# Attention gate and output projection of a two-layer trunk: order of the last gate tiles, of the output-weight splits and of the contraction blocks

## The chip, the cores and the metric

The kernel runs on one core of a Trainium2 chip. The metric is the device time of one execution in microseconds (us). Three executions of the kernel before took 1691.3 to 1694.68 us, their median is 1691.89 us. The profile comes from another execution.

## The reference

The program is a decoder trunk of two layers over 1024 tokens of width 1024, in float32. What the change touches is the end of layer 0:

```python
# layer 0: dilated attention, three dilation groups, 16 heads of 64
outs, lses = [], []
for g, (window, dilation) in enumerate(((128, 1), (512, 4), (2048, 16))):
    o, l = dilated_group_attention(q[g], k[g], v[g], rel_bias, window, dilation)
    outs.append(o); lses.append(l)
wts = softmax(stack(lses), axis=0)            # merge of the three groups
o = sum(wts[..., None] * stack(outs), axis=0)
h = (o * silu(z)) @ w_out                     # gate, then output projection
x = x + rms_norm(h, post_norm)
# layer 1: gated state-space layer, the same frame
```

The gate input z is a projection of the normalised input, like q, k and v.

## The kernel before

Each float32 operand of a large product is split into a rounded high part and a low part (`split`, L79: a copy on ScalarE, L83, and a subtraction on VectorE, L84), and each product is three matmuls: high by high, high by low, low by high. The contraction over 1024 goes in eight blocks k of 128.

Heads go in eight pairs p of 128 channels. For each pair the three groups are projected, attended and merged; the merge weights come from the row maxima and sums (`merge_weights`, L604: a load of them as tile `cm` at L609, small VectorE operations and an exponential on ScalarE, L612 to L620, and a store to `wt_dr`), and are loaded again as `mw` by `weights_of`. For pairs 0 to 6 the merge runs on GpSimd (`merge`, L684 to L690) and leaves the result in `on_dr`. For the last pair `merge_last` (L694) does it on VectorE, on tiles that are in SBUF.

The gate is projected in channel tiles p of 128 and token halves th of 512. Tiles 4 to 7 are projected early, in the first phase, and stored; the merges of pairs 4 to 6, and the last merge by L703, multiply by them. Tiles 0 to 3 are projected in `attn_gate`, whose work stands among and behind that of the last pair: `in_order` runs (0,0), (0,1), (1,0), (1,1), (2,0), (2,1), (3,0), (3,1). Each step makes a SiLU (`silu2`: tanh on ScalarE at L803, a product on VectorE at L804, tile `tz`), loads the merged heads (`fz`, L833), multiplies the two on GpSimd (L834) and splits the product into `gh` and `gl`. A gate product for half th fills half the columns of every token tile, so a block k is complete when both halves are done. Beside the first three steps `early` loads and splits blocks 4, 5 and 6 (L824). The tiles `tz` and `fz` come from one ring of seven slots under two tags (3 and 4), taken in turn by `slot`.

The output projection (`attn_out`, `out_tiles`) computes eight token tiles i by two column halves n. Its weights are loaded as `wo` (L815) and split into `woh` and `wol`. These tiles take the space of the attention's activations: column half 0 that of token half 0 (high parts under tag a0, low parts under a2), column half 1 that of token half 1 (a1 and a3). So a split of the weights of half n can begin only when the last projection has read token half n. `out_tiles` begins with four groups, (0,0), (1,0), (0,1), (1,1), over blocks 0 to 6, then adds block 7 to each, then takes the other tiles one by one, with the post norm (`out_norm`) and the next layer's normalised transposes beside them.

All loads and stores are issued on SyncE's queue. Every engine runs its queue in order. The order on each queue is made before the launch by a planner, which simulates the program with its own durations and takes what is ready, program order and the priority of `high_priority` deciding; so an instruction may stand elsewhere than the source has it. `issue_after(x)` makes it place an instruction behind x.

Of the kernel before, what the change touches and what calls it, by code (L numbers as in the profile page):

```python
# [18 lines left out]
AF = mybir.ActivationFunctionType  # L19
ALU = mybir.AluOpType  # L20
# [6 lines left out]
KT = 8  # L27
# [4 lines left out]
AHEAD = 600  # L32

EARLY = 4


ORD = (1, 4, 8)
# [41 lines left out]
def split(c, hi, lo, src, scale=None, engine=None):  # L79

    nc = c.nc
    if scale is None:
        nc.scalar.copy(hi, src)  # L83
        return (engine or nc.vector).tensor_tensor(lo, src, f32(hi), op=ALU.subtract)  # L84
    else:
        nc.scalar.activation(hi, src, AF.Copy, scale=scale)
        nc.vector.scalar_tensor_tensor(lo, src, scale, f32(hi), op0=ALU.mult, op1=ALU.subtract)
# [513 lines left out]
        nc.sync.dma_start(bass.AP(dr.tensor, off + n * 1024, dims), md[8 * n:8 * n + 8])  # L601


def merge_weights(c, p):  # L604

    nc = c.nc
    cm, e, d = c.compact
    src = bass.AP(c.ms_dr.tensor, c.ms_dr.offset + p * 3 * 4096, [[32, 64], [2048, 6], [1, 32]])
    nc.sync.dma_start(cm.rearrange("p g m n -> p (g m) n"), src)  # L609
    m, s = cm[:, :, 0], cm[:, :, 1]  # L610
    mx, den = d[:, 0], d[:, 1]
    nc.vector.tensor_tensor(mx, m[:, 0], m[:, 1], op=ALU.max)  # L612
    nc.vector.tensor_tensor(mx, mx, m[:, 2], op=ALU.max)
    nc.vector.tensor_tensor(e, m, mx.unsqueeze(1).to_broadcast([64, 3, 32]), op=ALU.subtract)
    nc.scalar.activation(e, e, AF.Exp)
    nc.vector.tensor_tensor(s, s, e, op=ALU.mult)
    nc.vector.tensor_tensor(den, s[:, 0], s[:, 1], op=ALU.add)
    nc.vector.tensor_tensor(den, den, s[:, 2], op=ALU.add)
    nc.vector.reciprocal(den, den)
    nc.vector.scalar_tensor_tensor(e, e, 0.5, den.unsqueeze(1).to_broadcast([64, 3, 32]), op0=ALU.mult, op1=ALU.mult)  # L620
    off = c.wt_dr.offset + p * 3 * 2048
    nc.sync.dma_start(bass.AP(c.wt_dr.tensor, off, [[32, 64], [2048, 3], [1, 32]]), e)
# [16 lines left out]
def attn_pair(c, p, w_in, h):  # L639
    nc = c.nc  # L640
    c.pair = p
    O = []
    for g in range(3):
        qh = c.attn.tile([P, S], F32R, tag="qh", name="qh", bufs=2)
        ql = c.attn.tile([P, S], F32R, tag="ql", name="ql", bufs=2)
        w = load_w(c, w_in[g * 8 + p])
        for th in range(2):
            src = proj_half(c, w, h[th])
            with c.tc.high_priority(AHEAD):
                evac_q(c, src, g, th * H, (qh, ql))  # L650
# [12 lines left out]
        ms = c.small.tile([P, 32], F32, tag="ms", name="ms")  # L663
        for u in range(2):
            attn_unit(c, g, u, (qh, ql), (kh, kl), v, bt, ms, O)
            if p and g == u == 0:
                merge_weights(c, p - 1)
    if p == 7:
        merge_weights(c, p)
        c.last = O  # L670
    c.merge = lambda: merge(c, p, O)

# [21 lines left out]
def merge_last(c, O, w):  # L694

    nc = c.nc
    for g in range(3):
        nc.vector.tensor_tensor(O[g], O[g], w[g], op=ALU.mult)
        if g:
            nc.vector.tensor_tensor(O[g], O[g], O[g - 1], op=ALU.add)  # L700
    g7 = c.wraw.tile([P, S], F32, tag="wraw", name="mg")
    nc.sync.dma_start(g7, c.g_dr[7])
    nc.vector.tensor_tensor(O[2], O[2], g7, op=ALU.mult)  # L703
    return O[2]
# [94 lines left out]
def silu2(c, t, ps):  # L799

    nc = c.nc
    with c.tc.high_priority(AHEAD):
        nc.scalar.activation(t, ps, AF.Tanh, scale=0.5)  # L803
        nc.vector.scalar_tensor_tensor(t, t, 1.0, ps, op0=ALU.add, op1=ALU.mult)  # L804


def attn_gate(c, a, h):
# [9 lines left out]
    def early(p):  # L817
        load_out(p, 0)
        for i in range(2):
            if p == 7:  # L820
                f = merged[:, i * H:i * H + H]
            else:
                f = c.slot("fz")
                nc.sync.dma_start(f, c.on_dr[p, :, i * H:i * H + H])  # L824
            split(c, g[i][0][:, p, :], g[i][1][:, p, :], f)

    def use(p, th, ps):
        if th == 0:
            load_out(p, 0)
        t = c.slot("tz")  # L830
        silu2(c, t, ps)
# [9 lines left out]
    def step(t):  # L841
        if t < 7 - EARLY:
            early(EARLY + t)
        c.wide = int(t >= 3)
        if t == 2 * EARLY - 2:
            with c.tc.high_priority(AHEAD):
                weights.extend(weights_of(c, 7, g) for g in range(3))

    in_order(c, [a["w_in"][48 + p] for p in range(EARLY)], h, use, step)
    c.wide = c.banks = 0  # L850
    merged = merge_last(c, c.last, weights)
    early(7)
    for p in range(8):
        load_out(p, 1)
    return g, raw
# [2 lines left out]
def out_part(c, ps, g, w, i, n, ks):  # L858
# [2 lines left out]
    gh, gl = g[i // 4]  # L861
    wh, wl = w[n]
    ts = slice(i % 4 * P, i % 4 * P + P)
    for k in ks:
        nc.tensor.matmul(ps, gh[:, k, ts], wh[:, k, :], start=k == 0, stop=False)  # L865
        nc.tensor.matmul(ps, gh[:, k, ts], wl[:, k, :], start=False, stop=False)  # L866
        nc.tensor.matmul(ps, gl[:, k, ts], wh[:, k, :], start=False, stop=k == KT - 1)  # L867


def out_bank(c, i):  # L870
# [1 line left out]
    return pool.tile([P, H], F32, tag=tag, name="pso")  # L872


def out_half(c, g, w, i, n):

    ps = out_bank(c, i)
    out_part(c, ps, g, w, i, n, range(KT))
    return ps


# [28 lines left out]
        done(ns)  # L910


def out_tiles(c, g, w, post, res, done, late=0, last=None):


    pss = [[None] * 2 for _ in range(8)]
    split_k = KT - 1 if late else KT
    order = [(0, 0), (1, 0), (0, 1), (1, 1)] if late < 3 else [(i, n) for n in range(2) for i in range(late)]
    for i, n in order:
        pss[i][n] = out_bank(c, i)  # L920
        out_part(c, pss[i][n], g, w, i, n, range(split_k))
    ahead = max(2, late)
    for i in range(8):
        if late and i == 0:
            for j in range(ahead):
                for n in range(2):
                    out_part(c, pss[j][n], g, w, j, n, (KT - 1,))
        elif i + 1 >= ahead and i < 7:
            for n in range(2):
                pss[i + 1][n] = out_half(c, g, w, i + 1, n)  # L930
# [16 lines left out]
def attn_out(c, a, g, raw):  # L947
# [527 lines left out]
def trunk(tc, a):  # L1475
# [6 lines left out]
    with ExitStack() as es:  # L1482
# [61 lines left out]
        for n in range(2):  # L1544
            for k in range(KT):
# [5 lines left out]
        out_tiles(c, y2, w, post, lambda i: c.x1_dr[i], lambda i, x: nc.sync.dma_start(ov[i], x), 2,  # L1551
                  lambda x, ns: nc.sync.dma_start(ov[7][:, ns], x[:, ns]))


# [88 lines left out]
```

## Time and profile before

| What | Value |
|---|---|
| median of 3 runs | 1691.89 us |
| profiled execution | 1692.35 us |
| its span, first to last instruction | 1690.6 us |
| mean granted TensorE clock | 0.991 |
| TensorE matmul, busy | 1655.9 us (98%) |
| VectorE, busy | 1012.3 us (60%) |
| ScalarE, busy | 712.8 us (42%) |
| GpSimd, busy | 452.8 us (27%) |

Times in the trace are microseconds from the start of the span. PE is TensorE's matmul, PEld its weight load, DVE VectorE, ACT ScalarE, POOL GpSimd, SP SyncE, which issues the transfers. A granted clock of 1.00 is TensorE's full speed. In rows of instructions, "out<-in" are the kernel's tiles, and a bracket or a last column tells how long the engine stood idle before it and who ended that. Merged rows (x6) give the start of the first and the time to the end of the last.

### The profile page before, as it was taken

What the parts mean: (1) busy time and instruction counts of PE and PEld (TensorE: products, weight loads), DVE (VectorE), ACT (ScalarE), POOL (GpSimd) and SP (SyncE); (2) the same over time, 40 slices, a digit from 0 to 9 for tenths busy, and PEclk for the clock granted to TensorE, in tenths of its full rate; (3) what the DMA queues carried; (4) which work ended last, traced back from release to release, by engine and by line L of the source; (5) the groups of instructions that cost most, each with busy time, mean ns of one, the idle gap of its engine ahead of it and who ended that gap; (6) DMA issues with size and microseconds to landing.
All of it is one profiled execution on the core that took longest, in us unless ns stands there. A gap on an engine that the chain in (4) does not pass through costs nothing.

```text
span 1690.6 us, 26330 instructions
## 1 busy us (share of the span) xinstructions
PE 1655.9 (98%) x9714; PEld 1395.1 (83%) x9714; DVE 1012.3 (60%) x2511; ACT 712.8 (42%) x1730; POOL 452.8 (27%) x301
## 2 busy tenths in 40 slices
PE   8999999999999999999999999998999999999998
PEld 6889999978888888888888888886888887867886
DVE  8698898625454554545455454567462788845533
ACT  5232232226456464646556464654352222243411
POOL 2000000132241514324252523303220344513121
PEclk9999999999999999999999999998999999989999
DMA  6222455531232423233142323228146978365432
GB/s 238 83 55 101 148 176 163 166 105 54 89 104 65 118 69 98 83 93 92 58 136 71 110 83 101 87 69 225 63 155 195 262 223 250 112 206 164 147 119 87
DMA packets 176857, 212.19 MB, mean 126 GB/s; under 512 B 37443, under 2 KB 133462, under 8 KB 176728
## 3 DMA queue, kind: packets, MB, share of 16 engines
q1 hardware_dynamic: 176728, 210.52, 41.7%
q8 instruction: 76, 1.25, 0.3%
q14 instruction: 53, 0.43, 0.1%
HBM read 153.51 MB, written 56.96 MB: 124 GB/s over the span
## 4 chain that ended last, share of the span: by engine, by line
PE 85%; DVE 7%; DMA 4%; issue 1%; POOL 1%; ACT 1%; SPq 0%; DVEq 0%; POOLq 0%; ACTq 0%
PE psj L110 45%; PE psq L373 10%; PE psl L471 5%; PE pso L548 4%; PE pt L499 4%; PE pso L865 3%; PE pso L866 3%; PE pso L867 3%; PE psb L110 1%; PE pso L574 1%; DVE T L1366 1%; DMA fz<-on_dr 1%; PE psv L234 1%; PE psv L233 1%; PE psv L232 1%
## 5 line engine op out<-in xcount | busy, mean ns | idle before, releaser
L110 PE MATMUL psj<-hh,whi 128*128 128x512 f32 x896 | 358.1, 400 | 0.0
L110 PE MATMUL psj<-hh,wlo 128*128 128x512 f32 x896 | 358.1, 400 | 0.0
L110 PE MATMUL psj<-hl,whi 128*128 128x512 f32 x896 | 355.2, 396 | 0.0
L84 POOL TENSOR_TENSOR wlo<-wraw,whi 128x1024 fp32r<-128x1024 f32 x48 | 115.2, 2400 | 394.8 <-ACT whi L83 379.7
L110 PEld LDWEIGHTS psj<-hh,whi 128*128 128x128 f32 x896 | 168.8, 188 | 37.0
L110 PEld LDWEIGHTS psj<-hh,wlo 128*128 128x128 f32 x896 | 168.8, 188 | 36.4
L110 PEld LDWEIGHTS psj<-hl,whi 128*128 128x128 f32 x896 | 168.7, 188 | 36.3
L488 ACT ACTIVATE lg<-lg,nm 128x128 f32<-128x128 f32 (+1 forms) x384 | 168.2, 442 | 37.0 <-DVE nm L483 37.0
L477 DVE CUSTOM_DVE_ANT_0 lg<-psl,T 128x128 f32<-128x128 f32 (+1 forms) x384 | 110.6, 347 | 89.1 <-PE psl L471 89.1
L83 ACT CAST whi<-wraw 128x1024 fp32r<-128x1024 f32 x80 | 83.7, 1046 | 161.9 <-PE psj L110 108.0
L373 PE MATMUL psq<-whi,v 128*128 128x256 f32 x640 | 120.3, 284 | 0.0
L110 PE MATMUL psj<-h1h,whi 128*128 128x512 f32 (+1 forms) x272 | 104.9, 386 | 1.1 <-ACT h1h L83 1.1
L84 DVE TENSOR_TENSOR ph<-pt,ph 128x512 fp32r<-128x512 f32 (+2 forms) x160 | 96.7, 622 | 15.3 <-ACT ph L83 13.1
L84 DVE TENSOR_TENSOR kl<-psj,kh 128x512 fp32r<-128x512 f32 x48 | 33.2, 691 | 119.3 <-ACT kh L83 118.8
L110 PE MATMUL psj<-h1l,whi 128*128 128x512 f32 (+1 forms) x272 | 104.2, 383 | 0.2 <-DVE h1l L84 0.2
L110 PE MATMUL psj<-h1h,wlo 128*128 128x512 f32 (+1 forms) x272 | 104.0, 383 | 0.0
L83 ACT CAST ph<-pt 128x512 fp32r<-128x512 f32 (+2 forms) x160 | 81.5, 529 | 46.5 <-PE pt L499 45.5
L373 PEld LDWEIGHTS psq<-whi,v 128*128 128x128 f32 x640 | 100.0, 189 | 1.2 <-issue 1.2
L373 PE MATMUL psq<-wlo,v 128*128 128x256 f32 x320 | 91.2, 285 | 0.7 <-DVE wlo L84 0.7
L548 PE MATMUL pso<-ph,vs 128*128 128x256 f32 (+1 forms) x544 | 86.6, 284 | 0.0
L499 PE MATMUL pt<-identr,lg 128*128 128x128 f32 x560 | 82.2, 276 | 0.0
L1232 POOL TENSOR_TENSOR Ks<-Ks,O 128x16 f32<-128x16 f32 x8 | 4.3, 536 | 284.5 <-ACT Ks L1230 284.5
(284 smaller groups left out, 3691.0 us busy)
## 6 DMA issues: line engine op xcount, KB each, us to landing
wraw<-in_w_in_dram SPq DMA_DIRECT2D x56, 512.0 KB
mw<-wt_dr SPq DMA_DIRECT2D x48, 256.0 KB
v<-in_w_v_dram SPq DMA_DIRECT2D x20, 512.0 KB
vp<-v_dr SPq DMA_DIRECT2D x16, 512.0 KB
wraw<-in_ssm_w_in_dram SPq DMA_DIRECT2D x16, 512.0 KB
v_dr<-v SPq DMA_DIRECT2D x30, 256.0 KB
rot_dr<-rt SPq DMA_DIRECT2D x48, 128.0 KB
ca_dr<-ca SPq DMA_DIRECT2D x32, 144.0 KB
```

What stands on the lines that cost most here:

```text
L83: nc.scalar.copy(hi, src)
L84: return (engine or nc.vector).tensor_tensor(lo, src, f32(hi), op=ALU.subtract)
L110: nc.tensor.matmul(ps, a[:, s], b[:, k, :], start=first and k == 0 and n == 0, stop=k == KT - 1 and n == 2, skip_group_check=True)
L373: nc.tensor.matmul(o, r[x][:, k, ts], w[y][:, k, :], skip_group_check=True, start=i in (0, 4, 5) and t % 2 == k == n == 0, stop=k == 3 and ...
L471: nc.tensor.matmul(psl[:, h, o], x[HEADS[h], qs], y[HEADS[h], ks], start=j == js[0] and n == 0, stop=n == 2, skip_group_check=True)
L477: nc.vector.tensor_tensor_reduce(lg[:, h, j, 0:w], psl[:, h, o], bt[:, h, 256 - w:256], scale=1.0, scalar=-3.0e38, op0=ALU.add, op1=ALU.ma ...
L488: nc.scalar.activation(lg[:, h, j, 0:w], lg[:, h, j, 0:w], AF.Exp, bias=nm[:, h, b:b + 1], accum_out=ms[:, col:col + 1])
L499: c.nc.tensor.transpose(pt[:, n * P:(n + 1) * P], lg[:, h, j, part * P:part * P + P], c.ident)
L548: nc.tensor.matmul(o, l, r, start=n == 0, stop=n == len(jobs) - 1, skip_group_check=True)
L865: nc.tensor.matmul(ps, gh[:, k, ts], wh[:, k, :], start=k == 0, stop=False)
L866: nc.tensor.matmul(ps, gh[:, k, ts], wl[:, k, :], start=False, stop=False)
L867: nc.tensor.matmul(ps, gl[:, k, ts], wh[:, k, :], start=False, stop=k == KT - 1)
```

## The change

It has five parts. The merge weights of the last pair: their load stays, the arithmetic moves into the second gate step, behind the splits of block 5. The gate steps run in the order (0,0), (0,1), (1,0), (1,1), (2,0), (3,0), (2,1), (3,1). The splits of the output weights go through the blocks in the order 4, 5, 6, 0, 1, 2, 3, 7, and those of column half 1 are placed behind the last SiLU. The output projection contracts in the same order of blocks, and its first four groups run over six blocks, with blocks 3 and 7 added after. The two additions of the last merge go to GpSimd. The output projection of layer 1 is called with the plain order of blocks and a split of seven and one, as it was before.

```diff
+K_GATED = (4, 5, 6, 0, 1, 2, 3, 7)
+K_ORDER = tuple(range(8))
...
-        nc.scalar.copy(hi, src)
+        c.last_hi = nc.scalar.copy(hi, src).ins
...
+def merge_load(c, p):
     cm, e, d = c.compact
     src = bass.AP(c.ms_dr.tensor, c.ms_dr.offset + p * 3 * 4096, [[32, 64], [2048, 6], [1, 32]])
-    nc.sync.dma_start(cm.rearrange("p g m n -> p (g m) n"), src)
+    c.nc.sync.dma_start(cm.rearrange("p g m n -> p (g m) n"), src)
...
     if p == 7:
-        merge_weights(c, p)
+        merge_load(c, p)
         c.last = O
...
         if g:
-            nc.vector.tensor_tensor(O[g], O[g], O[g - 1], op=ALU.add)
+            nc.gpsimd.tensor_tensor(O[g], O[g], O[g - 1], op=ALU.add)
...
-            split(c, g[i][0][:, p, :], g[i][1][:, p, :], f)
+            c.early_lo = split(c, g[i][0][:, p, :], g[i][1][:, p, :], f).ins
...
+        if t == 1:
+
+            with c.tc.issue_after(c.last_hi), c.tc.issue_after(c.early_lo):
+                merge_weights(c, 7)
...
-    in_order(c, [a["w_in"][48 + p] for p in range(EARLY)], h, use, step)
+    ws = {}
+    for t, (p, th) in enumerate(((0, 0), (0, 1), (1, 0), (1, 1), (2, 0), (3, 0), (2, 1), (3, 1))):
+        if th == 0:
+            ws[p] = load_w(c, a["w_in"][48 + p])
+        use(p, th, proj_half(c, ws[p], h[th]))
+        step(t)
     c.wide = c.banks = 0
     merged = merge_last(c, c.last, weights)
     early(7)
+    c.gates_done = c.silu
...
-    for k in ks:
-        nc.tensor.matmul(ps, gh[:, k, ts], wh[:, k, :], start=k == 0, stop=False)
+    for n, k in ks:
+        nc.tensor.matmul(ps, gh[:, k, ts], wh[:, k, :], start=n == 0, stop=False)
...
     for n in range(2):
-        for k in range(KT):
-            split(c, w[n][0][:, k, :], w[n][1][:, k, :], raw[n][:, k, :])
+        with ExitStack() as es:
+            if n:
+                for i in c.gates_done:
+                    es.enter_context(c.tc.issue_after(i))
+            for k in K_GATED:
+                split(c, w[n][0][:, k, :], w[n][1][:, k, :], raw[n][:, k, :])
...
-    out_tiles(c, g, w, post, lambda i: xv[i], done, 2)
+    out_tiles(c, g, w, post, lambda i: xv[i], done, K_GATED, 2)
```

## Rows read from the trace of the kernel before

**Rows 1.** The page: busy time by engine (us, share of the span, instructions), and the chain of work that ended last, by engine.

```profile
PE 1655.9 (98%) x9714; PEld 1395.1 (83%) x9714; DVE 1012.3 (60%) x2511; ACT 712.8 (42%) x1730; POOL 452.8 (27%) x301
...
PE 85%; DVE 7%; DMA 4%; issue 1%; POOL 1%; ACT 1%; SPq 0%; DVEq 0%; POOLq 0%; ACTq 0%
```

**Rows 2.** TensorE's groups of instructions from 1154.3 to 1261.9: line, tiles, shapes, count, then busy us, mean ns of one, idle us just before them and who ended it. `pso` is the output projection, `pst` the transposes.

```profile
L866 PE MATMUL pso<-wol,gh 128*128 128x512 f32 x128 | 52.9, 414 | 3.0 <-DVE wol L84 3.0
L865 PE MATMUL pso<-woh,gh 128*128 128x512 f32 x128 | 52.6, 417 | 3.9 <-ACT gh L83 3.9
L867 PE MATMUL pso<-woh,gl 128*128 128x512 f32 x128 | 49.9, 401 | 0.7 <-DVE gl L84 0.7
L127 PE MATMUL pst<-identr,xn 128*128 128x128 f32 x48 | 6.2, 272 | 0.0
```

**Rows 3.** Stretches of the span: bounds, length, then busy us (instructions) of PE, PEld, DVE, ACT and POOL in this order, the granted TensorE clock, the share of the 16 DMA engines, and GB/s.

```profile
1154.03:1261.95 107.92, 100.21 (x435) 80.38 (x434) 62.76 (x203) 47.15 (x108) 28.34 (x20) 0.95 0.39 128
1143.05:1154.25 11.20, 11.20 (x49) 9.01 (x48) 7.77 (x9) 4.47 (x9) 3.45 (x3) 1.00 1.11 247
1110.00:1130.00 20.00, 20.00 (x127) 16.94 (x127) 9.96 (x29) 11.94 (x40) 3.30 (x2) 1.00 0.05 15
1139.00:1171.00 32.00, 28.24 (x114) 21.98 (x113) 28.12 (x40) 16.52 (x33) 8.62 (x5) 0.95 1.10 309
...
1158.90:1162.10 3.20, 3.20 (x9) 2.47 (x9) 3.20 (x5) 2.91 (x7) 0.64 (x1) 0.50 1.02 382
1176.80:1182.50 5.70, 5.69 (x13) 4.51 (x14) 0.81 (x3) 0.27 (x1) 0.00 (x0) 0.50 0.00 0
```

**Rows 4.** TensorE's instructions in order of time, at full clock: start us, us, line, tiles. Between these two starts stand two further matmuls.

```profile
1183.58 0.40 PE L866 MATMUL pso<-wol,gh 128*128 128x512 f32 x1
...
1184.28 0.40 PE L866 MATMUL pso<-wol,gh 128*128 128x512 f32 x1
```

**Rows 5.** The chain of waits in order of time, around the gate and the output projection: start us, us, what.

```profile
1131.62 2.57 DMA cm<-ms_dr
...
1145.52 7.56 DMA fz<-on_dr
...
1163.83 7.30 DMA fz<-on_dr
...
1176.36 0.41 ACT gh L83
...
1178.04 0.43 PE pso L865
...
1209.17 0.87 PE pst L127 x8
```

**Rows 6.** ScalarE's instructions in order of time: start us, us, line, tiles, shapes, count, idle time before and who ended it.

```profile
1134.93 0.28 ACT L615 ACTIVATE cm<-cm 64x96 f32<-64x96 f32 x1 [2.76 <-DVE cm L614]
...
1135.37 3.41 ACT L83 CAST gh<-fz 128x256 fp32r<-128x256 f32 x8
```

**Rows 7.** GpSimd's instructions in order of time, the same columns.

```profile
1110.15 1.69 POOL L834 TENSOR_TENSOR fz<-fz,tz 128x512 f32<-128x512 f32 x1 [38.24 <-DVE tz L804]
1120.36 1.61 POOL L834 TENSOR_TENSOR fz<-fz,tz 128x512 f32<-128x512 f32 x1 [8.53 <-DVE tz L804]
...
1171.29 5.03 POOL L834 TENSOR_TENSOR fz<-fz,tz 128x512 f32<-128x512 f32 x2 [11.75 <-DMA fz<-on_dr]
```

**Rows 8.** VectorE's instructions in order of time, the same columns.

```profile
1137.47 3.15 DVE L84 TENSOR_TENSOR gl<-fz,gh 128x512 fp32r<-128x512 f32 x6
...
1152.35 1.22 DVE L698 TENSOR_TENSOR O<-O,mw 128x1024 f32<-128x1024 f32 x1
...
1156.69 6.41 DVE L84 TENSOR_TENSOR wol<-wo,woh 128x512 fp32r<-128x512 f32 x7
...
1172.19 1.28 DVE L84 TENSOR_TENSOR gl<-O,gh 128x512 fp32r<-128x512 f32 x2
1175.32 2.29 DVE L84 TENSOR_TENSOR gl<-fz,gh 128x256 fp32r<-128x256 f32 x4 [1.85 <-ACT gh L83]
```

**Rows 9.** Transfers issued on SyncE's queue, in order of time: start us, us of the issue, line, tiles, count.

```profile
1122.00 0.34 SPq L824 DMA_DIRECT2D fz<-on_dr  x1
...
1137.40 0.33 SPq L824 DMA_DIRECT2D fz<-on_dr  x1
...
1146.87 4.86 SPq L833 DMA_DIRECT2D fz<-on_dr  x2
...
1163.83 1.82 SPq L833 DMA_DIRECT2D fz<-on_dr  x2
```

**Rows 10.** Durations of single operations, by line or tile: ns min/median/max, first and last start us, shapes.

```profile
L83 ACT CAST woh<-wo x16: 612/618/627, 1151.9 to 1163.9; 128x512 fp32r<-128x512 f32 x16
...
L84 DVE TENSOR_TENSOR wol<-wo,woh x16: 675/677/2067, 1156.7 to 1171.6; 128x512 fp32r<-128x512 f32 x16
...
L700 DVE TENSOR_TENSOR O<-O,O x2: 1226/1900/2574, 1151.2 to 1153.6; 128x1024 f32<-128x1024 f32 x2
...
L834 POOL TENSOR_TENSOR fz<-fz,tz x8: 1516/1738/3557, 1110.1 to 1174.8; 128x512 f32<-128x512 f32 x8
...
L824 SPq DMA_DIRECT2D fz<-on_dr x6: 319/380/600, 877.4 to 1139.8; - x6
...
L686 POOL TENSOR_TENSOR O<-O,O x14: 2387/2393/2404, 477.8 to 1063.2; 128x1024 f32<-128x1024 f32 x14
```

More of the change, by code (lines that the diff above doesn't have):

```diff
@@ L601, in put_ms @@
         nc.sync.dma_start(bass.AP(dr.tensor, off + n * 1024, dims), md[8 * n:8 * n + 8])
+def merge_load(c, p):
+    cm, e, d = c.compact
+    src = bass.AP(c.ms_dr.tensor, c.ms_dr.offset + p * 3 * 4096, [[32, 64], [2048, 6], [1, 32]])
+    c.nc.sync.dma_start(cm.rearrange("p g m n -> p (g m) n"), src)
 def merge_weights(c, p):
@@ L607, in merge_weights @@
     cm, e, d = c.compact
-    src = bass.AP(c.ms_dr.tensor, c.ms_dr.offset + p * 3 * 4096, [[32, 64], [2048, 6], [1, 32]])
-    nc.sync.dma_start(cm.rearrange("p g m n -> p (g m) n"), src)
     m, s = cm[:, :, 0], cm[:, :, 1]
@@ L666, in attn_pair @@
             if p and g == u == 0:
+                merge_load(c, p - 1)
                 merge_weights(c, p - 1)
     if p == 7:
-        merge_weights(c, p)
+        merge_load(c, p)
         c.last = O
@@ L802, in silu2 @@
     with c.tc.high_priority(AHEAD):
-        nc.scalar.activation(t, ps, AF.Tanh, scale=0.5)
-        nc.vector.scalar_tensor_tensor(t, t, 1.0, ps, op0=ALU.add, op1=ALU.mult)
+        return (nc.scalar.activation(t, ps, AF.Tanh, scale=0.5).ins,
+                nc.vector.scalar_tensor_tensor(t, t, 1.0, ps, op0=ALU.add, op1=ALU.mult).ins)
 def attn_gate(c, a, h):
@@ L830, in use @@
         t = c.slot("tz")
-        silu2(c, t, ps)
+        c.silu = silu2(c, t, ps)
         f = c.slot("fz").rearrange("p (i n) -> p i n", i=8)
@@ L863, in out_part @@
     ts = slice(i % 4 * P, i % 4 * P + P)
-    for k in ks:
-        nc.tensor.matmul(ps, gh[:, k, ts], wh[:, k, :], start=k == 0, stop=False)
+    for n, k in ks:
+        nc.tensor.matmul(ps, gh[:, k, ts], wh[:, k, :], start=n == 0, stop=False)
         nc.tensor.matmul(ps, gh[:, k, ts], wl[:, k, :], start=False, stop=False)
-        nc.tensor.matmul(ps, gl[:, k, ts], wh[:, k, :], start=False, stop=k == KT - 1)
+        nc.tensor.matmul(ps, gl[:, k, ts], wh[:, k, :], start=False, stop=n == KT - 1)
 def out_bank(c, i):
@@ L872, in out_bank, with out_half @@
     return pool.tile([P, H], F32, tag=tag, name="pso")
-def out_half(c, g, w, i, n):
+def out_half(c, g, w, i, n, ks):
     ps = out_bank(c, i)
-    out_part(c, ps, g, w, i, n, range(KT))
+    out_part(c, ps, g, w, i, n, ks)
     return ps
@@ L910, in out_norm_last, with out_tiles @@
         done(ns)
-def out_tiles(c, g, w, post, res, done, late=0, last=None):
+def out_tiles(c, g, w, post, res, done, order, late, last=None):
     pss = [[None] * 2 for _ in range(8)]
-    split_k = KT - 1 if late else KT
-    order = [(0, 0), (1, 0), (0, 1), (1, 1)] if late < 3 else [(i, n) for n in range(2) for i in range(late)]
-    for i, n in order:
+    ks = list(enumerate(order))
+    for i, n in ((0, 0), (1, 0), (0, 1), (1, 1)):
         pss[i][n] = out_bank(c, i)
-        out_part(c, pss[i][n], g, w, i, n, range(split_k))
-    ahead = max(2, late)
+        out_part(c, pss[i][n], g, w, i, n, ks[:KT - late])
     for i in range(8):
-        if late and i == 0:
-            for j in range(ahead):
+        if i == 0:
+            for j in range(2):
                 for n in range(2):
-                    out_part(c, pss[j][n], g, w, j, n, (KT - 1,))
-        elif i + 1 >= ahead and i < 7:
+                    out_part(c, pss[j][n], g, w, j, n, ks[KT - late:])
+        elif i < 7:
             for n in range(2):
-                pss[i + 1][n] = out_half(c, g, w, i + 1, n)
+                pss[i + 1][n] = out_half(c, g, w, i + 1, n, ks)
         x = c.wraw.tile([P, D], F32, tag="wraw", name="xr")
@@ L1550, in trunk @@
         ov = a["out"].rearrange("(n i) d -> i n d", i=8)
-        out_tiles(c, y2, w, post, lambda i: c.x1_dr[i], lambda i, x: nc.sync.dma_start(ov[i], x), 2,
+        out_tiles(c, y2, w, post, lambda i: c.x1_dr[i], lambda i, x: nc.sync.dma_start(ov[i], x), K_ORDER, 1,
                   lambda x, ns: nc.sync.dma_start(ov[7][:, ns], x[:, ns]))
```

## The prediction

> **What bounds the kernel now.** I read the page's busy times and chain of waits first: TensorE is busy for 98% of the span and holds 85% of the chain [rows 1], so an edit counts only where it closes a hole in TensorE's stream or lifts its clock. Next, TensorE's groups between the last gate projection and the second layer: three waits stand there, of 3.0, 3.9 and 0.7 us, all in the first matmuls of the attention's output projection [rows 2]. What this stage is worth follows from a sum. From its first weight load (1154.03) to the next layer's first projection (1261.95) are 107.92 us [rows 3]. Its 384 output matmuls at 0.23 us (0.233 as the mean of three in 0.70) take 89.5, its 48 transposes at 0.87 per eight take 5.2 [rows 2, 4, 5]. So 13.2 us are lost. Of these 7.6 are the three waits. Another 4.1 is clock: for 3.2 us and 5.7 us after two of the waits the granted clock is 0.50, the 1.2 GHz level [rows 3], where a matmul takes 0.43 instead of 0.23 [rows 4, 5], so 46% of 8.9 us. The remaining 1.5 is refilling around the waits. 13.2 us is the most that this stage can give back.
>
> Who ends the waits is read from the chain in time [rows 5]. The small transfer of the merge's row sums ends at 1134.2. On ScalarE the merge's exponential stands at 1134.93 with 2.76 us of idle before it, and eight casts of gated blocks stand behind it [rows 6]. Their inputs were in long before: two products of gate tile 0 ended on GpSimd by 1122 [rows 7]. The subtractions that free their ring slots end at 1140.6 [rows 8]. From there the chain is ring slot, load, product, cast, slot: loads of 7.56 and 7.30 us among them, the last issued at 1163.83, because the subtraction that frees its slot stands behind seven output-weight subtractions, 1156.69 to 1163.1 [rows 5, 8, 9]. The last gate product ends at 1176.3 and its cast at 1176.8 lets TensorE go on. The transfers are slow because the 16 DMA engines are full from 1139 to 1171 (share 1.10), though from 1110 to 1130 they were nearly idle (0.05) [rows 3].
>
> **The change, part by part.**
>
> *Merge weights behind the early blocks.* The arithmetic (eight small VectorE operations and one exponential) moves behind the splits of block 5; only its load stays. So the eight casts (3.41 us) and their subtractions no longer wait for 1134.2. Of the six loads of blocks 4 to 6 two were issued from 1137 on, so the fourth, block 5's second, is the one of 1122.00 [rows 9, 10], and its split can be done by about 1126, before the row sums land: the merge itself need not be later. At best ring slots come free some 12 us earlier, and the loads now issued at 1137 to 1148 run while the DMA engines are idle; at worst the planner, which orders the engines by its own times, leaves the order as it is and nothing is gained. I take most of the best, since the data are there.
>
> *Token halves.* The projections run (2,0), (3,0), (2,1), (3,1). Half 0 of the activations is then read for the last time two projections (2 x 24 x 0.233 = 11.2 us) before the end, at about 1143, instead of one (1148.7). Output weights of columns 0 to 511 are written into the space of that half. Now seven of their low parts come after 1156.69 [rows 8] and TensorE waits 3.0 us for the first. Their cost is 8 x 0.62 on ScalarE and 8 x 0.68 on VectorE [rows 10]; from 1143.05 to 1154.25 ScalarE is busy for 4.47 of 11.20 us and VectorE for 7.77 [rows 3]. So ScalarE's 5.0 fit, VectorE's 5.4 find 3.4 and overrun by about 2, but TensorE takes 4.2 us over the first 18 matmuls, in which the rest can follow. Value: between 0 (no slot used) and the whole 3.0 and its 1.5 of clock. I take the larger part. The loads of tile 3's weights stand one projection earlier on SyncE's queue; no wait of TensorE in this stage is for such a load [rows 2], so 0.
>
> *Columns 512 to 1023 behind the last SiLU.* An added wait, on ScalarE's tanh and VectorE's product of the last gate tile. Queued behind it are 16 splits. They can start at about 1156, and TensorE needs the first after two groups of 18 matmuls at 1154.25 + 8.4 = 1162.65. From then a block is wanted each 0.70 us and made each 0.68. Cost none while no other work of VectorE stands between; if the cover is gone, 0.68 per block. The gate's subtractions are no longer behind them, which frees the last ring slot.
>
> *Blocks 3 and 7 last.* Four groups of six blocks, 72 matmuls, 16.8 us, run before either is needed: to 1171.05. Block 7 is complete now at 1173.5 and block 3 at 1177.6 [rows 8], with the casts at 1176.4 in the chain [rows 5]. Even unmoved, that leaves a wait of 5.8 us; with loads earlier by the 12 us above it leaves none. The block order inside a group costs nothing.
>
> *Additions on GpSimd.* Two at 1.23 us leave VectorE, two of 2.39 (the same shape in earlier pairs) come to GpSimd [rows 7, 8, 10]. Beside GpSimd VectorE's operations stretch: the second addition took 2.57 beside a gate product, an output-weight subtraction up to 2.07 instead of 0.68 [rows 10]. So VectorE's bill is between -2.5 and +2.3 (4.8 of blocking less 2.5); I take 0, since part of the additions will meet VectorE idle. Block 7's chain gets 2.4 us longer, against a slack of about ten. The Trainium skill ("SBUF — State Buffer", section "SBUF: two separate sides") says that the ports VectorE and GpSimd share are an exclusive lock, held for a whole instruction, also against VectorE operations with two SBUF inputs. The trace agrees (2.57 against 1.23 us). By that rule in full, VectorE's stream here is 2.3 us longer, and if that stream set the end of the stage the gain below would be 5.9 us, 1686.0.
>
> *The last stage of the kernel* (same split of 7 and 1 blocks, same order) is unchanged: 0.
>
> **The sum.** The three causes go, but several deadlines stand close together after 1154, so I leave one wait of the mean size (7.6/3 = 2.5), one stretch of low clock of the mean size (2.05) and 0.5 of refilling: 5.0 remain of 13.2, a gain of 8.2. Behind this stage TensorE's stream is dense, so the gain goes through to the end. The profiled execution took 1692.35 (span 1690.6): 1684.15. The median of the runs shown lies 0.46 lower: 1683.7.
>
> **Rivals.**
>
> *The last gate tile is late all the same* (17%). If its loads keep waiting for a slot, its cast stays at 1176.8. TensorE waits 5.8 from 1171.05, plus 2.6 of clock and 0.5: 8.9 of 13.2 stay, gain 4.3, 1687.6. For it speaks that ring slots are still seven; against it that each link of the chain that delayed them is moved.
>
> *The transfers bound the stage* (12%). The full DMA stretch ends at about 1171 and carries 309 GB/s for 32 us, 9.9 MB. If the output weights, wanted from 1154 on, still land as late as about 1160 and the rest of the queue with them, TensorE trades a late wait for an early one: gain about 1, 1690.9. Against it: the block and gate loads that are issued at 1137 to 1148 now [rows 9] can leave the full stretch, as far as the slots come free earlier.
>
> *Slower: the merge queues behind the gate products* (9%). GpSimd runs its queue in order, and the second addition may stand behind the last gate product. If that product still ends at 1176.3, the addition ends at 1178.7, and with blocking (a product took 3.56 instead of 1.52 beside VectorE's stream [rows 7]) at 1180.7; product with the gate 1.2, cast 0.6, subtraction 0.7 make block 7 ready at 1183.2. TensorE then loses 12.2 + 2.6 + 0.5 = 15.3, 2.1 more than now: 1694.0. It decides from block 7 ready at 1181.1 (13.2 - 3.1 after 1171.05) on. Against it: merge products end at 1153.6 [rows 8], well before.
>
> **How the numbers follow.** The forecast has 62%, with its own range from no loss left (gain 13.2) to a gain of 5: 1678.7 to 1686.9. 0.2% (3.4 us) is about what a measurement can tell from no change. Faster by more than that: the forecast and most of the first rival, 76%. Within: the rest of it and the second, 15%. Slower: the third, with what the planner may disturb elsewhere, 9%. The range of 1679.5 to 1691.0 leaves out the third, part of the second and the very best.
>
> **What would show it.** Right: casts of gated blocks before 1130 on ScalarE; no load of a gate tile issued after about 1157; output-weight subtractions before 1154; the first 72 output matmuls without a wait of over 1 us and a granted clock of 1.00 through them. Wrong: a wait of TensorE of 5 us or more before block 3 or 7, or again two stretches at 0.50; DMA full beyond 1165 with gate loads in it.

## The result and the profile after

The changed kernel takes 1682.38 us (median of four runs, 1679.3 to 1683.09) against 1692.29 us of the kernel before (four runs, 1691.3 to 1694.68): a ratio of 0.994 with a 95% interval of 0.9925 to 0.9955. That is 9.9 us less, where 8.2 were forecast. The profiled execution is the fastest of the four, 1679.3 us with a span of 1677.5.

The page first: busy times of the engines (us, share, instructions), and the chain of work that ended last.

```profile
PE 1650.1 (98%) x9714; PEld 1390.6 (83%) x9714; DVE 1011.9 (60%) x2509; ACT 712.2 (42%) x1730; POOL 460.0 (27%) x303
...
PE 87%; DVE 7%; DMA 3%; issue 1%; POOL 1%; ACT 1%; SPq 0%; DVEq 0%; ACTq 0%; POOLq 0%
```

Beside [rows 1] TensorE issues the same 9714 matmuls and is busy 5.8 us less; 4.5 of this lie in the stage below (100.21 against 95.67 us), where it ran fewer of them at the lower clock. The other engines' totals tell nothing of the gain.

The ruler for all that follows is the stage: from the last matmul of the gate projections (its start and 0.23 us) to the first matmul of layer 1. In the kernel before that is 1154.25 to 1261.79, 107.5 us. TensorE's instructions of the changed kernel in order of time give the other end (start us, us, line, tiles, and in brackets the idle time before and who ended it):

```profile
1152.53 0.39 PE L113 MATMUL psj<-hh,wlo 128*128 128x512 f32 x1
1152.76 0.40 PE L884 MATMUL pso<-woh,gh 128*128 128x512 f32 x1
...
1172.66 0.40 PE L885 MATMUL pso<-wol,gh 128*128 128x512 f32 x1
1173.87 0.50 PE L884 MATMUL pso<-woh,gh 128*128 128x512 f32 x1 [0.81 <-ACT gh L86]
...
1176.03 0.50 PE L886 MATMUL pso<-woh,gl 128*128 128x512 f32 x1 [1.20 <-DVE gl L87]
...
1250.14 0.39 PE L113 MATMUL psj<-h1h,whi 128*128 128x512 f32 x1
```

From 1152.76 to 1250.14 are 97.4 us, so the stage gives 10.1 of the gain. The spans differ by 13.1; of the other 3.0, 1.5 us are gone before this stage begins (its start moved from 1154.25 to 1152.76) and 1.4 come after it (from the stage's end to the end of the span are 428.8 us before and 427.4 after). Over the eleven further runs these two lengths vary by more than that (starts from 1152.9 to 1156.8, 425.4 to 430.6 us behind the stage), so nothing is read into them.

TensorE's groups in the stage, to be laid beside [rows 2] (busy us, mean ns of one, idle us and its releaser):

```profile
L884 PE MATMUL pso<-woh,gh 128*128 128x512 f32 x128 | 50.6, 397 | 0.8 <-ACT gh L86 0.8
L885 PE MATMUL pso<-wol,gh 128*128 128x512 f32 x128 | 50.4, 395 | 0.0
L886 PE MATMUL pso<-woh,gl 128*128 128x512 f32 x128 | 50.4, 400 | 1.2 <-DVE gl L87 1.2
```

Three waits of 7.7 us in all have become two of 2.0, and none is for an output weight. The mean of one matmul says the same of the clock: 395 to 400 ns, where the kernel before has 401 to 417. Stretches of the span (bounds, length, busy us and count of PE, PEld, DVE, ACT and POOL, granted clock, DMA share, GB/s), beside [rows 3]:

```profile
1152.45:1250.14 97.69, 95.67 (x436) 77.08 (x435) 61.87 (x196) 44.15 (x103) 32.76 (x23) 1.00 0.43 136
...
1165.00:1175.00 10.00, 9.02 (x38) 6.50 (x36) 5.67 (x9) 0.71 (x2) 7.72 (x4) 1.00 0.93 277
...
1173.50:1179.00 5.50, 3.93 (x16) 2.92 (x17) 4.46 (x5) 1.76 (x4) 2.19 (x1) 1.00 0.54 178
```

The clock is 1.00 through the whole stage, also in the 5.5 us around the two waits. The matmuls and transposes alone take 94.7 us by the prediction's sum, so 2.7 us are still lost, where the prediction left 5.0 (from the first weight load, 1152.45, as the prediction measured, it is 3.0).

What the other engines do is the surprise. ScalarE in order of time, beside [rows 6]:

```profile
1133.59 0.37 ACT L582 COPY O<-pso 64x256 f32<-64x256 f32 x1 [2.92 <-PE pso L577]
1133.86 3.41 ACT L86 CAST gh<-fz 128x256 fp32r<-128x256 f32 x8
...
1142.31 0.28 ACT L622 ACTIVATE cm<-cm 64x96 f32<-64x96 f32 x1 [1.35 <-DVE cm L621]
...
1142.97 3.22 ACT L86 CAST woh<-wo 128x512 fp32r<-128x512 f32 x6
...
1154.33 4.26 ACT L86 CAST woh<-wo 128x512 fp32r<-128x512 f32 x8
...
1173.41 0.71 ACT L86 CAST gh<-fz 128x256 fp32r<-128x256 f32 x2 [9.71 <-POOL fz L842]
```

The exponential has moved from in front of the eight casts to 8.5 us behind their start, and yet they start 18.9 us before the end of the gate projections (1152.76 - 1133.86), exactly as before (1154.25 - 1135.37). What stands directly before them is a copy of attention's last result. In the trace of the kernel before, the same copy stood in the place that [rows 6] leaves out, and the matmuls that it waited for ended almost together with the exponential; TensorE and ScalarE of the kernel before:

```profile
1134.30 0.75 PE L574 MATMUL pso<-ph,vs 128*128 128x256 f32 x5
```

```profile
1135.12 0.35 ACT L579 COPY O<-pso 64x256 f32<-64x256 f32 x1
```

The matmuls end at 1135.05, the exponential at 1135.21: two possible releasers 0.2 us apart, and the profile's chain [rows 5] goes by the merge arithmetic, the later one. `gh`, `gl` and `wo` lie in a pool that is opened after the attention's pools are closed. The loads of `wo`, on another queue, need nothing but room, and they begin as these matmuls end (1135.08 before, 1133.59 in the changed kernel). SyncE's waits, first before, then after (who waited for whom: us in all, times, longest):

```profile
SPq L815 <- PE pso L574: 2.8, 1, 2.8
```

```profile
SPq L823 <- PE pso L577: 2.8, 1, 2.8
```

So the loads wait for the room that attention's last matmuls give free. The casts of `gh` write into the same pool and stand directly behind the copy of these matmuls' result: whether they wait for the room or for their place behind the copy, what ends the wait is attention, not the exponential.

SyncE's queue (start us, us of the issue, line, tiles, count), beside [rows 9]:

```profile
1149.83 7.96 SPq L841 DMA_DIRECT2D fz<-on_dr  x3
1157.88 3.81 SPq L642 DMA_DIRECT2D mw<-wt_dr  x6
1165.97 0.55 SPq L841 DMA_DIRECT2D fz<-on_dr  x1
```

The six loads of the merge weights, 256 KB each, were issued at 1141.74 before, among the output weights' loads; they now come at 1157.88, after the last of those. The last load of a gate tile is still late: 13.2 us after the gate projections' end; before, the last two went out 9.6 to 11.4 us after it. VectorE and GpSimd, beside [rows 8] and [rows 7]:

```profile
1134.45 3.84 DVE L87 TENSOR_TENSOR gl<-fz,gh 128x256 fp32r<-128x256 f32 x8
...
1145.15 0.67 DVE L87 TENSOR_TENSOR wol<-wo,woh 128x512 fp32r<-128x512 f32 x1
...
1157.73 6.38 DVE L87 TENSOR_TENSOR wol<-wo,woh 128x512 fp32r<-128x512 f32 x8
...
1165.50 1.42 DVE L87 TENSOR_TENSOR gl<-fz,gh 128x256 fp32r<-128x256 f32 x4
...
1173.85 2.46 DVE L87 TENSOR_TENSOR gl<-fz,gh 128x256 fp32r<-128x256 f32 x2 [4.33 <-ACT gh L86]
...
1178.14 1.30 DVE L87 TENSOR_TENSOR gl<-O,gh 128x512 fp32r<-128x512 f32 x2 [0.69 <-ACT gh L86]
```

```profile
1168.13 3.64 POOL L708 TENSOR_TENSOR O<-O,O 128x1024 f32<-128x1024 f32 x1 [1.65 <-DVE O L706]
1171.74 1.64 POOL L842 TENSOR_TENSOR fz<-fz,tz 128x512 f32<-128x512 f32 x1
1173.32 2.37 POOL L708 TENSOR_TENSOR O<-O,O 128x1024 f32<-128x1024 f32 x1
```

The output weights' low parts begin 11.5 us earlier. Counted from the start of the stage, block 3 is ready no earlier than before (23.5 us after it, at 1176.3, against 23.4) and block 7 is 7.5 us later (26.7, at 1179.4, against 19.2). The supply of the last blocks has not become faster; TensorE has other work meanwhile, and all but 2.0 us of the lateness is hidden. The last gate product has no idle time before it: it stood behind an addition.

### The profile page after: what moved, and what is told of

It reads as the page before. It is cut to its first block, busy times and chain, and to the rows that moved or that the text cites. A ratio compares the mean times of both kernels' runs of the same rounds, so it can differ in the third digit from the quotient of the medians.

```text
span 1677.5 us, 26337 instructions
## 1 busy us (share of the span) xinstructions
PE 1650.1 (98%) x9714; PEld 1390.6 (83%) x9714; DVE 1011.9 (60%) x2509; ACT 712.2 (42%) x1730; POOL 460.0 (27%) x303
## 4 chain that ended last, share of the span: by engine, by line
PE 87%; DVE 7%; DMA 3%; issue 1%; POOL 1%; ACT 1%; SPq 0%; DVEq 0%; ACTq 0%; POOLq 0%
PE psj L113 46%; PE psq L376 11%; PE psl L474 5%; PE pso L551 4%; PE pt L502 4%; PE pso L886 3%; PE pso L885 3%; PE pso L884 3%; PE pso L577 1%; PE psb L113 1%; DVE T L1387 1%; PE psv L237 1%; DVE T L1392 1%; PE psv L236 1%; PE psv L235 1%
## 5 line engine op out<-in xcount | busy, mean ns | idle before, releaser
L87 DVE TENSOR_TENSOR ph<-pt,ph 128x512 fp32r<-128x512 f32 (+2 forms) x160 | 96.7, 622 | 15.3 <-ACT ph L86 13.1
```

## The experiments

All the kernels of the table compute the whole result. "Stage" is the length defined above and "idle" TensorE's waits in it, both from each run's profile; medians are of the runs without profile and with it, and every ratio is to the kernel before on the same chip.

| run | median us (runs) | ratio, 95% interval | stage | idle |
|---|---|---|---|---|
| kernel before | 1692.29 (4) | 1 | 107.5 | 7.7 |
| changed kernel | 1682.38 (4) | 0.994 [0.9925, 0.9955] | 97.4 | 2.0 |
| changed_again | 1683.12 (5) | 0.9951 [0.9937, 0.9965] | 97.3 | 2.0 |
| undo_merge_move | 1684.04 (5) | 0.9962 [0.9949, 0.9976] | 100.1 | 4.9 |
| undo_token_halves | 1684.89 (5) | 0.9967 [0.9954, 0.9979] | 98.5 | 2.5 |
| undo_block_order | 1687.84 (11) | 0.9982 [0.9973, 0.9991] | 103.1 | 6.0 |
| undo_gpsimd_add | 1678.58 (5) | 0.9935 [0.9922, 0.9947] | 96.5 | 1.2 |
| undo_gpsimd_add_again | 1679.76 (6) | 0.9941 [0.9929, 0.9954] | 96.1 | 1.0 |
| only_block_order | 1683.53 (4) | 0.9958 [0.9942, 0.9973] | 100.4 | 3.5 |
| only_token_halves | 1689.75 (10) | 0.9991 [0.9981, 1.0002] | 108.0 | 8.8 |
| early_weights_late_products | 1684.05 (6) | 0.9958 [0.9944, 0.9972] | 98.6 | 3.1 |
| early_weights_late_loads | 1684.32 (4) | 0.9962 [0.9947, 0.9976] | 103.5 | 6.1 |
| late_loads_add_on_vectore | 1679.84 (5) | 0.9942 [0.993, 0.9953] | 96.8 | 1.3 |

The two profiles of the changed kernel agree within 0.1 us in the stage, the two without additions on GpSimd within 0.4, while medians of one kernel differ by up to 1.2. So differences of 1 us between variants are read from the stage and from what ends its waits, and the medians say no more than the direction.

**The merge arithmetic back in its old place.**

```diff
     if p == 7:
         merge_load(c, p)
+        merge_weights(c, p)
...
-        if t == 1:
-
-            with c.tc.issue_after(c.last_hi), c.tc.issue_after(c.early_lo):
-                merge_weights(c, 7)
```

> The changed kernel, but the merge weights of the last pair are computed where they were, at the end of the pair. Theory of the prediction (the move frees the ring slots earlier): the gated loads come later, TensorE waits again for block 3, 3 to 5 us more than the changed kernel, about 1686, the stage from the last gate projection to the first projection of layer 1 at 101 to 103 instead of 97.7 us. Rival (the casts of the blocks wait for the space that the attention's last tiles hold, not for the exponential): casts start at 1134 to 1135 as in both kernels, the stage stays at 97 to 98.5, the time within 1 us of the changed kernel, and block 7 is ready some 6 us earlier without use.

The stage is 2.7 us longer than the changed kernel's, between the two expected ranges, so the move does pay. But not by the casts: ScalarE has them again 18.9 us before the end of the gate projections (1152.87), with the exponential now ahead of them and done in time. What is new stands 20 us later on the same engine:

```profile
1133.37 0.28 ACT L622 ACTIVATE cm<-cm 64x96 f32<-64x96 f32 x1 [2.59 <-DVE cm L621]
1133.71 0.37 ACT L582 COPY O<-pso 64x256 f32<-64x256 f32 x1
1133.97 3.41 ACT L86 CAST gh<-fz 128x256 fp32r<-128x256 f32 x8
...
1153.95 0.62 ACT L86 CAST woh<-wo 128x512 fp32r<-128x512 f32 x1 [6.94 <-DMA wo<-in_w_out_dram]
```

ScalarE waits 6.94 us for an output weight, and SyncE's queue of this run tells why it is late:

```profile
1140.73 3.68 SPq L642 DMA_DIRECT2D mw<-wt_dr  x6
...
1145.76 8.51 SPq L824 DMA_DIRECT2D wo<-in_w_out_dram  x9
```

The merge weights' 1.5 MB go ahead of the ten output weights that are left, nine of them in this row. Early arithmetic means early loads, and these the move puts back. TensorE's waits in this run are 2.33 us for a low part of an output weight and, the longer one, 2.61 us for the low part of a gated block (until 1162.10). VectorE and GpSimd there:

```profile
1159.48 4.36 DVE L87 TENSOR_TENSOR gl<-fz,gh 128x256 fp32r<-128x256 f32 x2
```

```profile
1156.12 5.65 POOL L709 TENSOR_TENSOR O<-O,O 128x1024 f32<-128x1024 f32 x2
```

The two subtractions take 4.36 us beside the additions on GpSimd; the pair at 1150.33 of the changed kernel took 0.75. So the 2.7 us are not shown to come of the late weights alone: part of them may hang on where the additions run, and no run has the rest of the change with the merge's loads early and the additions on VectorE. Three later runs take the rest apart.

**The old order of the gate steps.**

```diff
-    for t, (p, th) in enumerate(((0, 0), (0, 1), (1, 0), (1, 1), (2, 0), (3, 0), (2, 1), (3, 1))):
+    for t, (p, th) in enumerate(((0, 0), (0, 1), (1, 0), (1, 1), (2, 0), (2, 1), (3, 0), (3, 1))):
```

> The changed kernel with the gate steps in the old order (2,0), (2,1), (3,0), (3,1). Theory (the token halves free the space of the first weight half one projection earlier): first output-weight casts 5.6 us later, a wait of 2 to 3.5 us at the first output matmuls and a stretch of low clock behind it; stage 101 to 103 us, time 1685.5 to 1688. Rival (the order of the blocks alone gives enough to do): stage under 99 us, time within 1 us of the changed kernel.

The stage is 1.2 us longer, as the rival has it and not the theory, though the median is 2.5 us higher. The casts of the output weights begin at 1151.1 instead of 1143.0, as the theory has it, but no wait of TensorE comes of that; its 2.5 us are for a gated block. The subtractions that follow start at 1151.85 and run on, where before three products and two additions of the merge stood ahead of them until 1156.69 [rows 8]; in this run the first of those products comes at 1162.21. So with the merge out of the way the splits keep ahead of TensorE even when they start only 2 us before it.

**The old order of the blocks,** with the old split of seven and one.

```diff
-            for k in K_GATED:
+            for k in range(KT):
...
-    out_tiles(c, g, w, post, lambda i: xv[i], done, K_GATED, 2)
+    out_tiles(c, g, w, post, lambda i: xv[i], done, K_ORDER, 1)
```

> The changed kernel with blocks in plain order 0 to 7 and only block 7 split off, as before. Theory: block 3 is complete at about 1176 in the changed kernel and is then wanted from the third to the tenth matmul on of every group, so TensorE waits and its clock falls; stage 104 to 107 us, time 1688 to 1692. Rival (token halves alone carry the gain): stage under 100 us, time under 1685.

The costliest part to lose: 5.7 us of stage. TensorE's waits in it:

```profile
1160.27 0.50 PE L885 MATMUL pso<-wol,gh 128*128 128x512 f32 x1 [0.64 <-DVE wol L87]
1166.63 0.50 PE L884 MATMUL pso<-woh,gh 128*128 128x512 f32 x1 [2.60 <-ACT gh L86]
1175.38 0.49 PE L884 MATMUL pso<-woh,gh 128*128 128x512 f32 x1 [2.74 <-ACT gh L86]
```

Two waits for gated blocks come back. The stage lies a little below the expected range, with a mean granted clock of 0.98.

**Each of these two alone on the kernel before.** `only_block_order` makes the last edit forward and `only_token_halves` the one ahead of it; neither has anything else of the change.

> The kernel before with the new block order and blocks 3 and 7 last, and nothing else. If the parts add up: it gives back what leaving it out costs (5.7 us of stage): 101 to 103 us instead of 107.5, with the wait of 3 us for the first weights and its low clock still there. Rival (it pays only together with the token halves): 105 us or more.

> The kernel before with the gate steps by token halves, and nothing else. Theory: the wait of 3 us for the first weights and one stretch of low clock go, block 3 stays late: stage 103 to 106 us. Rival (as leaving them out cost 1.2 us only, they give about 1 alone): 106 to 107.

Their groups of TensorE in the stage, first the block order alone, then the token halves alone:

```profile
L882 PE MATMUL pso<-wol,gh 128*128 128x512 f32 x128 | 51.9, 408 | 3.5 <-DVE wol L87 3.5
L881 PE MATMUL pso<-woh,gh 128*128 128x512 f32 x128 | 50.9, 402 | 0.0
L883 PE MATMUL pso<-woh,gl 128*128 128x512 f32 x128 | 50.7, 403 | 0.0
```

```profile
L881 PE MATMUL pso<-woh,gh 128*128 128x512 f32 x128 | 52.8, 415 | 8.8 <-ACT gh L86 8.8
L882 PE MATMUL pso<-wol,gh 128*128 128x512 f32 x128 | 52.7, 412 | 0.0
```

The block order alone takes the stage to 100.4, 7.1 of the 10.1 us and more than expected, and leaves just one wait, for the output weights' low parts. The token halves alone remove exactly that wait and bring nothing (108.0, outside both expected ranges): TensorE arrives sooner at the gated blocks and stands there for 8.8 us instead of 3.9 and 0.7. The two parts work in series on one stream, and only the later deadline counts.

**The additions back on VectorE.**

```diff
-            nc.gpsimd.tensor_tensor(O[g], O[g], O[g - 1], op=ALU.add)
+            nc.vector.tensor_tensor(O[g], O[g], O[g - 1], op=ALU.add)
```

> The changed kernel with both additions of the last merge on VectorE. Theory of the prediction: 0, within 1 us of the changed kernel, since VectorE saves 2.5 us and loses as much beside GpSimd. Rival by the shared port: the additions on GpSimd cost more than they save, so this kernel is 1 to 3 us faster and block 7 is ready 2 to 4 us earlier. Second rival: VectorE is the tight engine and this kernel is 1 to 3 us slower.

> The changed kernel with both additions on VectorE once more: stage 96 to 97 us as before; time 1680 to 1682.5.

In both profiles the stage is shorter than in the changed kernel, by 0.9 and 1.2 us, and both medians are lower, though the intervals of the ratios overlap with the changed kernel's. GpSimd in the second:

```profile
1170.13 2.64 POOL L842 TENSOR_TENSOR fz<-fz,tz 128x512 f32<-128x512 f32 x1 [2.98 <-DMA fz<-on_dr]
```

The last gate product starts when its load lands, 16.3 us after the end of the gate projections (1153.86; 16.7 in the first profile). In the changed kernel it starts 19.0 us after, behind an addition of 3.64 us. Block 3 is ready 21.7 and 21.3 us after that end here, 23.5 in both profiles of the changed kernel. But TensorE waits no longer for a cast in the changed kernel (0.81) than here (0.55 and 0.65 in the first, 1.04 in the second): the delay by the first addition is hidden behind matmuls. What TensorE feels is the second addition. Its wait of 1.20 in the changed kernel is for the subtraction that starts at 1173.85, and the view of tile `fz` from 1164 to 1176 shows what became of it (ns min/median/max, first and last start):

```profile
L87 DVE TENSOR_TENSOR gl<-fz,gh x8: 410/411/2129, 1164.0 to 1175.9; 128x256 fp32r<-128x256 f32 x8
```

Seven of eight subtractions take 0.41 us, this one 2.13: it lies beside the addition of 1173.32, which ends at 1175.69, and itself ends 0.3 us later. In the two runs without the additions on GpSimd TensorE has no wait for a low part. Together the additions cost about 1 us; no run moves just one of them.

**The changed kernel again,** as a base on the chip of the next runs.

> The changed kernel once more, beside the next ones: the stage from the last gate projection to the first projection of layer 1 at 97 to 98.5 us, the time at 1680 to 1683.

**What the merge's move is worth, taken apart.** First the arithmetic early, the merge's products and the split of block 7 behind the last output-weight split:

```diff
+        merge_weights(c, p)
...
-    merged = merge_last(c, c.last, weights)
-    early(7)
+    def finish():
+        merged = merge_last(c, c.last, weights)
...
+    with c.tc.issue_after(lo):
+        c.finish()
```

> The merge weights of the last pair are computed at the end of the pair, as before the change, but the merge's products on VectorE are placed behind the last split of the output weights. Theory (what the moved merge weights pay is only that the merge's three products come behind the weight splits on VectorE): no wait for a low part of the weights, stage 96.5 to 98.5 as in the changed kernel, against 100.1 with the early products. Rival (early merge weights cost by something else, such as their loads among the output weights): stage 99.5 to 101, a wait for the weights of over 1.5 us stays.

The stage is 98.6, just above the theory's range: better than with everything early (100.1), not as good as the changed kernel (97.4). ScalarE still waits 6.22 us for an output weight, since the loads of the merge weights stand at 1142.04, and TensorE waits 1.9 us for a low part. By these lengths the order of the products on VectorE, with the additions that follow them on GpSimd, is worth some 1.5 us, and the other 1.2 lie with what this kernel still has early, loads and arithmetic.

Then the arithmetic early and only the six loads behind the last load of an output weight:

```diff
+        merge_weights(c, p)
...
-            with c.tc.high_priority(AHEAD):
-                weights.extend(weights_of(c, 7, g) for g in range(3))
...
+        last = load_out(p, 1).ins
+    with c.tc.issue_after(last):
+        weights.extend(weights_of(c, 7, g) for g in range(3))
```

> The merge weights of the last pair are computed at the end of the pair, as before the change; their six loads (1.5 MB) are placed behind the last load of the output weights instead of among them. Theory (what the moved arithmetic of the merge weights pays is that these loads come behind the output weights): ScalarE's wait of 6 to 7 us for an output weight goes, stage 96.5 to 98.5 us as in the changed kernel, against 100.1 with early loads. Rival (it pays because of VectorE's order): stage 99.5 to 101.

A miss: 103.5. The wait for output weights is gone as expected (the `woh` casts run in three groups from 1143.54 and in a last one of eight from 1154.73 to 1158.99, none behind a transfer), but TensorE waits 6.1 us for gated blocks. GpSimd shows where they were:

```profile
1166.01 1.90 POOL L843 TENSOR_TENSOR fz<-fz,tz 128x512 f32<-128x512 f32 x1 [2.54 <-DMA fz<-on_dr]
1167.87 2.85 POOL L709 TENSOR_TENSOR O<-O,O 128x1024 f32<-128x1024 f32 x1
1170.67 1.73 POOL L843 TENSOR_TENSOR fz<-fz,tz 128x512 f32<-128x512 f32 x1
1173.96 2.39 POOL L709 TENSOR_TENSOR O<-O,O 128x1024 f32<-128x1024 f32 x1 [1.56 <-DVE O L707]
1176.31 1.69 POOL L843 TENSOR_TENSOR fz<-fz,tz 128x512 f32<-128x512 f32 x1
```

Each of the last two gate products stands behind an addition, the last until 1176.31, and the subtractions behind them on VectorE are stretched, too (the `gl` pair from 1168.38 takes 4.30 us, in the changed kernel at 1150.33 0.75). The same kernel with the additions on VectorE parts the two causes:

> As the kernel before this one, and both additions of the last merge on VectorE. Theory (the additions on GpSimd hold up the last gate product): 0.5 to 1.5 us less of stage than with them on GpSimd, 95.5 to 97 us, and the fastest of all runs, 1680 to 1682. Rival (the additions on VectorE come in the way of the weight splits): 97 us or more.

96.8, 6.7 us less by that one edit where 0.5 to 1.5 were expected, and as good as `undo_gpsimd_add` within 0.3 to 0.7. These two differ in where the merge arithmetic stands and in how the loads are held back. With the loads late and the additions off GpSimd, the place of the arithmetic is worth little or nothing.

## Why the prediction was right, point by point

The direction, the size and the general reason, that TensorE's waits go and nothing behind gives the gain back, came as forecast: 8.2 forecast, 9.9 by the medians, 10.1 in the stage. The way to it did not, and that the size came so near is in part luck: the step that was to free the ring slots 12 us earlier did not, and the order of the blocks brought more than was put down for it. The sum of what remains was 2.5 of waiting, 2.05 of low clock and 0.5 of refilling; measured are 2.0, none, and 0.7 (97.4 - 94.7 - 2.0). The clock is the term that was mis-sized: 2.05 us were put down for a stretch behind the wait that was left, and the two waits of 0.81 and 1.20 brought none.

*Merge weights behind the early blocks.* This step failed. "The eight casts and their subtractions no longer wait for 1134.2" and the ring slots 12 us earlier did not come: the casts stand at the same distance from the stage, with the exponential ahead of them or 8.5 us behind, and their subtractions end 14.5 us ahead of the stage instead of 13.6, not 12 us sooner. The reading took the later of two releasers 0.2 us apart, the one on the profile's chain, and did not ask what stood between exponential and casts. That the casts themselves wait for the attention's space is read from the code and from the loads of `wo`; no run here tests it. The part still pays (2.7 us in the changed kernel), with the merge's loads and products behind the output weights. That the early loads make the output weights late is shown by ScalarE's wait: 6.94, 6.22 and 6.75 us in the three kernels with early loads and the new order of gate steps (the third is `only_token_halves`), and none in those with the loads late. How much of the 2.7 us is that alone stays open, since the variant that moves just the loads made other waits and the longer wait without the part is for a subtraction beside an addition on GpSimd. "The merge itself need not be later" was wrong as well: block 7 is ready 7.5 us later in the stage.

*Token halves.* The low parts come earlier, as said. The value taken, the larger part of 3.0 + 1.5, is not there alone: 108.0 against 107.5. In the whole it is 1.2. The term counted a wait of TensorE without the one behind it, which grows by as much.

*Columns 512 to 1023 behind the last SiLU.* No wait of TensorE is for these weights, as said. What the part is worth is not known, since no run leaves out just this. The freed ring slot did not come: the subtraction that frees it is among the four at 1165.50, whose first casts ended by 1159.8, and it still stands behind all eight splits of these columns (1157.73 to 1164.11) and a product of the merge. That is why the last gate load goes out at 1165.97.

*Blocks 3 and 7 last.* Under-sized, and the reason why the failed first step did not matter: alone 7.1 of 10.1 us. By the step, a block 3 that comes no sooner leaves a wait of 5.8 us. It came no sooner in the stage (its last cast 1.5 us earlier, its last low part not at all), and TensorE waited 2.0. The step reckoned TensorE fed to 1171.05, by 72 matmuls. It ran without a wait to 1172.66 + 0.23, and (1172.66 - 1152.76) / 0.233 + 1 are 86 matmuls: the planner also took 14 of a further group, over blocks that were there. So TensorE had 20.1 us of work that needs neither block, not 16.8. This reserve was not in the prediction.

*Additions on GpSimd.* Taken as 0 within -2.5 to +2.3; measured about +1 us (0.9 and 1.2), within the bounds. A gate product starts 2.2 to 2.7 us later behind the first addition, in GpSimd's queue, but TensorE's wait for it did not grow; the subtraction that TensorE waits for takes 2.13 instead of 0.41 beside the second addition, and that wait, 1.20 us, is the cost. The stretching agrees with the rule of shared ports that the prediction took from the Trainium skill ("SBUF — State Buffer", section "SBUF: two separate sides"). The first addition, too, is 1.27 longer than the second (3.64 and 2.37), with a product of 1.21 on VectorE meanwhile. But the 1686.0 that went with the rule's full price did not come: VectorE's stream as a whole did not set the end, and of its operations TensorE waited for that one subtraction.

*The rivals.* The last gate tile is late all the same, the first rival's condition, and held: its last load goes out at 1165.97, when none was forecast after about 1157. Its price did not: 2.0 us of waiting instead of 5.8, since the cast let TensorE go on at 1173.87, not 1176.8, and TensorE had the 14 further matmuls. Of the second rival the sign is there (DMA share 0.93 from 1165 to 1175, with a gate load in it), but no wait of TensorE is for a transfer. The third rival's queue is there turned round, a gate product behind an addition. With the stretched subtractions it goes with about 1 us in the change and 6.7 in `early_weights_late_loads` (the 3.56 us of that rival stand in [rows 10], not [rows 7]).

Of the four signs that would show the steps right, two came (low parts of output weights before 1154, at 1145.15; no wait and a clock of 1.00 through the first 72 matmuls), and two did not (casts before 1130; no late gate load). A forecast can be right in its sum with a wrong first step, where a later step makes the deadline loose enough.

## What to carry to other kernels

When a contraction waits for its last operands, first move the late blocks to its end and let independent groups run ahead: here that took 7 of 10 us by itself, while a faster supply in front of the next deadline took nothing. When the profile names a releaser, look at the instruction directly ahead and at what else ended within a few tenths of a microsecond, before counting on the wait to go. An operation moved to a less busy engine still stands in that engine's queue: leave critical products nothing to stand behind; here the three runs with both additions on VectorE and the merge's loads late are the best of all (stage 96.1 to 96.8, 1678.58 to 1679.84 us).

## What the runs showed of the hardware

Waits of 0.81 and 1.20 us left TensorE's granted clock at 1.00 (1173.5 to 1179), where waits of 3.0 and 3.9 us in the kernel before were each followed by a stretch at 0.50 [rows 3]; with one wait of 3.5 us in all, in `only_block_order`, the stage has a mean of 0.97. But the length of a wait does not settle it: in `undo_block_order` the wait of 2.60 us was followed by 0.50 (1168 to 1170) and the longer one of 2.74 by 1.00 (1175.3 to 1183), and in `undo_merge_move` waits of 2.61 and 2.33 left 1.00 throughout. In the kernel before, 4.1 us of clock came with 7.7 of waiting; in the changed kernel both are back but for 2.0 us of waiting.

What is loaded early is not free where the transfer engines are full: in `undo_merge_move`, with a DMA share of 1.09 from 1140.73 to 1154, six loads of 256 KB issued at 1140.73 ahead of ten output weights went with a wait of 6.94 us for one of these, although block 7, which the merge serves, was wanted some 20 us later.

Beside a GpSimd addition of 2.37 us a VectorE subtraction took 2.13 us instead of 0.41, and ended 0.3 us after it; an addition beside a VectorE product of 1.21 us took 3.64 instead of 2.37.
